# A hybrid decoder block on one core: weights rounded by casting DMAs, remainders made by accumulating DMAs

## The chip, the core and the metric

One NeuronCore of a Trainium2 chip runs the whole kernel. The time is device microseconds of one execution; a kernel's time is the median of several. Engines are named as in the profile: PE is TensorE, DVE is VectorE, ACT is ScalarE, POOL is GpSimd, and SP issues DMAs alone.

## The reference

One decoder layer works on 512 tokens of width 1024 (x is 512x1024, float32):

```python
h = rmsnorm(x, ln_mix_g)
aq, ak, av, iq, ik, iw, hq, hf, hi, hg, cb, cc, ch, gates = split(h @ w_in)
y_attn = sparse_attention(rms(aq), rms(ak), av, top-k by relu(iq @ ik) * iw, rel_bias)   # 8 heads of 64
y_hgrn = rms(gated_recurrence(hq, hf, hi)) * silu(hg)                                     # 4 heads of 128
y_conv = cb * causal_conv3(cc * ch)                                                       # 512 channels
mixed  = sum over b of sigmoid(gates[b]) * (y_b @ w_up_b)
x = x + mixed @ w_out
x = x + relu(rmsnorm(x) @ w_mlp_up)**2 @ w_mlp_down                                       # width 4096
```

All weights are float32 and the products are wanted at about that precision.

## The kernel before

**Products in three parts.** A float32 operand a is split into a rounded part (type `F32R`) and a remainder: a = hi + lo. Every large product is hi·hi + hi·lo + lo·hi, three matmuls that add into one accumulator bank. Activations are split where they are made (`xh`/`xl`, `x2h`/`x2l`, `hh`/`hl`, `mh`/`ml`, `yp`); weights are split on the way in.

**Slabs.** The weights are laid out in 142 slabs of up to 128x1024 floats (512 KB) in the order in which they are used (`PLAN`, `slabs_of`, lines 32 to 63): `kv` (three slabs), `hf`, `hq`, `hi`, `aq`, `cc`/`ch`/`cb`, `hg`, then for each branch the gates `g2`, `g1`, `g0` with the up-projections `u2`, `u1`, `u0`, then `wo`, and twice 16 slabs `up` and 16 slabs `dn`. A full slab feeds 24 matmuls of 512 columns. In the first stage (`start`, accumulators `Ast`) the weights of `iq` and of `hf` 0 come in by chunks of their own (`wst`) and are split in `first`; the change leaves that alone.

**How a slab comes in.** `loader` (line 394) has SP issue a DMA of the slab into a `raw` tile (two of them). `splitter` (line 440) lets ScalarE round it into a `whi` tile and VectorE subtract, `wlo = raw - whi` (three tiles of each). Then both are handed to the stream of matmuls under the key `("w", n)`, and freed when its last matmul is issued.

**How the order is made.** Each engine's instructions stand in an order that a planner writes down while the program is built (`Order`, line 95). Generators (`loader`, `splitter`, the evacuations `ev_*`, `scan_task`, `soft_task`, `out_task` and so on) yield operations with a cost in ns (`Op`), `Get` a tile, or `Need` a key. The main stream of matmuls (`main`: `start`, `cols`, `rows`, `tall`) advances the planner's clock; another generator's step is taken when the planner believes its inputs to be ready, and DMAs on SP count as ready 2000 ns after they end. So costs in the source decide where an instruction stands; each engine then runs its own list strictly in order and waits on semaphores.

**Names around the change.** `Akv`, `Ahf`, `Ag`, `Au`, `Awo`, `Aup`, `Adn` are accumulators of the stages; there are five banks for these. `xt` are four blocks of x in eight tiles, whose squares (`stats`) give the row norms `R`; every evacuation of a projection needs `R`. `iqs` is the split of the first two `Ast` banks, which are free only after it. In the scan, ScalarE makes an exponential `Am`, GpSimd multiplies it by `KQ` (`scan_task`, line 848), and TensorE uses it (`pa`, or by way of `prd` in `psum`). The attention adds bias and mask on GpSimd (`cmb`), makes logits (`pl`), transposes the probabilities `p` (`pt`) and multiplies by the values (`po`).

Of the kernel before, what the change touches and what calls it, by code (L numbers as in the profile page):

```python
# [11 lines left out]
F32 = mybir.dt.float32  # L12
F32R = mybir.dt.float32r
U32 = mybir.dt.uint32
I32 = mybir.dt.int32
AF = mybir.ActivationFunctionType
# [49 lines left out]
class Op:  # L66
    __slots__ = ("e", "c", "ins", "outs", "f")

    def __init__(self, e, c, ins, outs, f):
        self.e, self.c, self.f = e, c, f  # L70
        self.ins = [key(a) for a in ins if not isinstance(a, (int, float, type(None)))]
        self.outs = [key(a) for a in outs if a is not None]
# [22 lines left out]
class Order:  # L95
# [41 lines left out]
    def run(self, op):  # L137
# [3 lines left out]
        if op.e == "D":  # L141
            end += 2000
# [107 lines left out]
def kernel(ctx: ExitStack, tc: tile.TileContext, xT, x, wst, slabs, vecs, rel, ident_d, masks_d,  # L250
# [9 lines left out]
    def maker(pool, tag, shape, n):  # L260
# [6 lines left out]
        ("raw", sp, (128, 1024), 2), ("whi", sp, (128, 1024), 3), ("wlo", sp, (128, 1024), 3),  # L267
# [126 lines left out]
    def loader():  # L394
# [8 lines left out]
        for n in range(NSL):  # L403
            r = yield Get("raw", "raw")
            w = SLABS[n][2] * SLABS[n][4]
            yield dma(r[:, :w], slabs[n][:, :w], nbytes=1 << 19)
            put(("raw", n), r)
# [32 lines left out]
    def splitter():  # L440
        for n in range(NSL):
            r = yield Need(("raw", n))
            _, _, nk, _, nc_ = SLABS[n]
            w = nk * nc_
            h = yield Get("whi", "whi", F32R)
            yield act(h[:, :w], r[:, :w], AF.Copy)
            l = yield Get("wlo", "wlo", F32R)
            yield tt(l[:, :w], r[:, :w], h[:, :w].bitcast(F32), ALU.subtract)
            free(r)
            put(("w", n), (h, l, h[:, :w].rearrange("p (k c) -> p k c", k=nk), l[:, :w].rearrange("p (k c) -> p k c", k=nk)))  # L450
# [622 lines left out]
    def cols(n, m0, name, ev, rhs):  # L1073

        h, l, h3, l3 = yield Need(("w", n))
        nk, c = SLABS[n][2], SLABS[n][4]
        for mt in range((c + 127) // 128):
            w = min(128, c - 128 * mt)
            ps = yield Get("acc", "A" + name)
            cs = slice(128 * mt, 128 * mt + w)  # L1080
            for k in range(nk):
                yield Need(rhs[0](k))
                bh, bl = rhs[1](k)
                yield [mm(ps[:w], h3[:, k, cs], bh, k == 0, False), mm(ps[:w], h3[:, k, cs], bl, False, False),
                       mm(ps[:w], l3[:, k, cs], bh, False, k == nk - 1)]
# [3 lines left out]
    def rows(n0, cnt, name, ev, lhs, ncol):  # L1089
# [3 lines left out]
        for i in range(cnt):  # L1093
            h, l, h3, l3 = yield Need(("w", n0 + i))
# [49 lines left out]
    def tall(n, f, m):  # L1144
        ps = yield Get("acc", "Adn")
        for i in range(2):
            h, l, h3, l3 = yield Need(("w", n + i))
            for k in range(8):
                bh, bl = yield Need(("h", 16 * f + 8 * i + k))
                yield [mm(ps, h3[:, k], bh, i + k == 0, False), mm(ps, h3[:, k], bl, False, False),  # L1150
                       mm(ps, l3[:, k], bh, False, i == 1 and k == 7)]
# [129 lines left out]
```

## Time and profile before

| | |
|---|---|
| median of 3 runs | 888.13 us (886.86 to 889.04) |
| the profiled execution | 887.85 us, span of its instructions 886.1 us |
| TensorE matmul busy | 866.7 us (98%) |
| VectorE / ScalarE / GpSimd busy | 564.5 / 353.8 / 151.4 us |
| DMA | 88.08 MB, 100 GB/s over the span |

A page's busy time of an engine is the time in which at least one of its instructions ran. Matmuls overlap, so the start of one to the start of the next says more than the duration of one. The table by stretches gives for each engine the busy time and in brackets the number of instructions, then the granted clock of TensorE (1.00 is full), the share of time in which the 16 DMA engines were busy, and GB/s. A wait is shown as engine, line, and after the arrow what ended it.

### The profile page before, as it was taken

Reading aid. Unit: us, or ns where it says so; the run is one execution under the profiler, and the core shown is the slowest. Engines: PE = TensorE matmul, PEld = TensorE weight load, DVE = VectorE, ACT = ScalarE, POOL = GpSimd, SP = SyncE. Lnnn points to the kernel's source line nnn. Section 1 sums busy time; section 2 is a strip of 40 time slices with the busy share of each in tenths; the row PEclk is TensorE's granted clock in tenths of the full one; section 3 lists DMA queues with packets and bytes.
Section 4 is the critical chain, followed back from the end, with each engine's and each line's share of the span. In section 5 each row is a group of like instructions: output and inputs, shape, how many; then the busy total and the mean of one; then the engine's idle time right before and its main releaser. Section 6 shows DMA issues by size and latency. Waiting matters only on the chain.

```text
span 886.1 us, 10647 instructions
## 1 busy us (share of the span) xinstructions
PE 866.7 (98%) x4060; PEld 719.7 (81%) x4060; DVE 564.5 (64%) x972; ACT 353.8 (40%) x562; POOL 151.4 (17%) x129
## 2 busy tenths in 40 slices
PE   7999999998999999999999999999999999999997
PEld 6888888787888888888877888888888888888886
DVE  5589899999999996686557546444333344444331
ACT  6664354334433455565563333333222133331110
POOL 0010146445422421162200130000011100000000
PEclk9999999999999999999999999999999999999999
DMA  8443321222222222222221522223322222223330
GB/s 292 160 138 139 113 78 71 72 95 72 72 90 81 92 72 72 72 72 80 88 71 53 199 100 77 95 95 98 116 95 95 95 95 95 95 96 119 121 116 25
DMA packets 27611, 88.08 MB, mean 99 GB/s; under 512 B 2928, under 2 KB 5800, under 8 KB 27560
## 3 DMA queue, kind: packets, MB, share of 16 engines
q1 hardware_dynamic: 27528, 87.38, 29.0%
q8 instruction: 32, 0.52, 0.3%
q14 instruction: 19, 0.16, 0.1%
q0 software_dynamic: 32, 0.02, 0.0%
HBM read 85.28 MB, written 3.68 MB: 100 GB/s over the span
## 4 chain that ended last, share of the span: by engine, by line
PE 92%; DVE 6%; ACT 1%; DMA 0%; issue 0%; ACTq 0%; POOLq 0%
PE Aup L334 20%; PE Adn L334 20%; PE Ag L334 15%; PE Au L334 7%; PE Awo L334 5%; PE Aaq L334 2%; PE Ahq L334 2%; PE Ahi L334 2%; PE Ahf L334 2%; PE Ahg L334 2%; PE Ast L334 2%; PE pa L334 2%; PE Ach L334 2%; PE Akv L334 2%; PE Acc L334 1%; PE pl L334 1%
## 5 line engine op out<-in xcount | busy, mean ns | idle before, releaser
L296 ACT ACTIVATE whi<-raw 128x1024 fp32r<-128x1024 f32 (+2 forms) x150 | 153.8, 1026 | 276.9 <-PE Adn L334 124.5
L300 DVE TENSOR_TENSOR wlo<-raw,whi 128x1024 fp32r<-128x1024 f32 (+2 forms) x150 | 199.5, 1331 | 60.6 <-ACT whi L296 59.9
L334 PE MATMUL Aup<-x2h,whi 128*128 128x512 f32 x256 | 100.0, 391 | 0.0
L334 PE MATMUL Aup<-x2h,wlo 128*128 128x512 f32 x256 | 99.6, 389 | 0.0
L334 PE MATMUL Aup<-x2l,whi 128*128 128x512 f32 x256 | 99.6, 389 | 0.0
L334 PE MATMUL Adn<-hh,whi 128*128 128x512 f32 x256 | 99.6, 389 | 0.0
L334 PE MATMUL Adn<-hl,whi 128*128 128x512 f32 x256 | 99.6, 389 | 0.0
L334 PE MATMUL Adn<-hh,wlo 128*128 128x512 f32 x256 | 99.6, 389 | 0.0
L300 DVE TENSOR_TENSOR rl<-rl 128x512 f32<-128x512 f32 x32 | 22.2, 692 | 96.4 <-ACT hh L296 96.4
L334 PE MATMUL Ag<-xhi,whi 128*128 128x512 f32 x192 | 77.8, 405 | 0.0
L334 PE MATMUL Ag<-xhi,wlo 128*128 128x512 f32 x192 | 75.3, 392 | 0.0
L334 PE MATMUL Ag<-xlo,whi 128*128 128x512 f32 x192 | 75.0, 391 | 0.0
L334 PE MATMUL Au<-yp,whi 128*128 128x512 f32 x192 | 61.8, 403 | 2.3 <-ACT yp L296 2.1
L296 ACT ACTIVATE rl<-Aup 128x512 f32<-128x512 f32 x32 | 19.1, 598 | 110.2 <-PE Aup L334 110.2
L300 POOL TENSOR_TENSOR Am<-Am,KQ 128x512 f32<-128x512 f32 x28 | 43.5, 1554 | 97.0 <-ACT Am L296 92.0
L334 PEld LDWEIGHTS Aup<-x2h,whi 128*128 128x128 f32 x256 | 48.0, 188 | 10.3 <-issue 0.2
L334 PEld LDWEIGHTS Aup<-x2l,whi 128*128 128x128 f32 x256 | 48.1, 188 | 10.1 <-issue 0.2
L334 PEld LDWEIGHTS Adn<-hh,wlo 128*128 128x128 f32 x256 | 48.0, 188 | 10.0
L334 PEld LDWEIGHTS Adn<-hh,whi 128*128 128x128 f32 x256 | 48.0, 188 | 10.0
L334 PEld LDWEIGHTS Aup<-x2h,wlo 128*128 128x128 f32 x256 | 48.0, 188 | 9.9
L334 PEld LDWEIGHTS Adn<-hl,whi 128*128 128x128 f32 x256 | 48.0, 188 | 9.9
L334 PEld LDWEIGHTS Au<-yp,whi 128*128 128x128 f32 x192 | 35.8, 192 | 9.6 <-ACT yp L296 2.2
(261 smaller groups left out, 1702.9 us busy)
## 6 DMA issues: line engine op xcount, KB each, us to landing
raw<-in_slabs_dram SPq DMA_DIRECT2D x139, 512.0 KB, 3.2
xt<-in_x_dram SPq DMA_DIRECT2D x8, 256.0 KB, 6.5
x<-in_xT_dram SPq DMA_DIRECT2D x4, 512.0 KB, 5.8
out_dram<-o SPq DMA_DIRECT2D x7, 256.0 KB, 2.0
xin<-in_xT_dram SPq DMA_DIRECT2D x3, 512.0 KB, 6.0
d<-d SPq DMA_DIRECT2D x1, 1536.0 KB
raw<-in_wst_dram SPq DMA_DIRECT2D x3, 384.0 KB, 4.5
toep<-d SPq DMA_DIRECT2D x1, 1024.0 KB, 5.6
```

The costliest lines, as they stand in the source:

```text
L296: return Op("A", c, [in_, scale, bias], [out_, accum], lambda: A.activation(out_, in_, func, **kw))
L300: return Op(e, c, [a, b], [out_], lambda: (V if e == "V" else G).tensor_tensor(out_, a, b, op))
L334: return Op("PE", c, [a, b] + ([] if start else [ps]), [ps], lambda: PE.matmul(ps, a, b, start=start, stop=stop))
```

## The change

A slab's tile `raw` is gone. `loader` has GpSimd issue a DMA that reads the slab in DRAM as float32 and writes it into a `whi` tile as `F32R`, so that the rounding happens on the way. `splitter` hands that tile on at once under the key `("wh", n)`, lets ScalarE write the negated copy, `wlo = -whi`, and has GpSimd issue a second DMA of the same slab that adds into `wlo`, which makes it w - hi; this is handed on under `("wl", n)`. VectorE has no part in it. There are five tiles of each kind. `cols` and `tall` first do all products with the rounded weights of a slab and then those with the remainders; `rows` keeps its order. The planner books 900 ns on GpSimd for either DMA, and 3500 or 4000 ns more until it counts as landed. The scratch in SBUF for such DMAs' descriptors is made smaller (4096 bytes of a partition) to make room.

```diff
 class Op:
-    def __init__(self, e, c, ins, outs, f):
-        self.e, self.c, self.f = e, c, f
+    def __init__(self, e, c, ins, outs, f, lat=0):
+        self.e, self.c, self.f, self.lat = e, c, f, lat
...
-        if op.e == "D":
-            end += 2000
+        end += 2000 if op.e == "D" else op.lat
...
-        ("raw", sp, (128, 1024), 2), ("whi", sp, (128, 1024), 3), ("wlo", sp, (128, 1024), 3),
+        ("whi", sp, (128, 1024), 5), ("wlo", sp, (128, 1024), 5),
...
     def loader():
...
-            r = yield Get("raw", "raw")
+            h = yield Get("whi", "whi", F32R)
             w = SLABS[n][2] * SLABS[n][4]
-            yield dma(r[:, :w], slabs[n][:, :w], nbytes=1 << 19)
-            put(("raw", n), r)
+            yield Op("G", 900, [], [h], lambda h=h, n=n, w=w: nc.gpsimd.dma_start(h[:, :w], slabs[n][:, :w]), 3500)
+            put(("raw", n), h)
...
     def splitter():
         for n in range(NSL):
-            r = yield Need(("raw", n))
+            h = yield Need(("raw", n))
             _, _, nk, _, nc_ = SLABS[n]
             w = nk * nc_
-            h = yield Get("whi", "whi", F32R)
-            yield act(h[:, :w], r[:, :w], AF.Copy)
+            put(("wh", n), (h, h[:, :w].rearrange("p (k c) -> p k c", k=nk)))
             l = yield Get("wlo", "wlo", F32R)
-            yield tt(l[:, :w], r[:, :w], h[:, :w].bitcast(F32), ALU.subtract)
-            free(r)
-            put(("w", n), (h, l, h[:, :w].rearrange("p (k c) -> p k c", k=nk), l[:, :w].rearrange("p (k c) -> p k c", k=nk)))
+            yield act(l[:, :w], h[:, :w].bitcast(F32), AF.Copy, scale=-1.0)
+            yield Op("G", 900, [l], [l], lambda l=l, n=n, w=w: nc.gpsimd.dma_start(
+                l[:, :w], slabs[n][:, :w], accum_op=ALU.add), 4000)
+            put(("wl", n), (l, l[:, :w].rearrange("p (k c) -> p k c", k=nk)))
...
     def tall(n, f, m):
         ps = yield Get("acc", "Adn")
         for i in range(2):
-            h, l, h3, l3 = yield Need(("w", n + i))
+            h, h3 = yield Need(("wh", n + i))
             for k in range(8):
                 bh, bl = yield Need(("h", 16 * f + 8 * i + k))
-                yield [mm(ps, h3[:, k], bh, i + k == 0, False), mm(ps, h3[:, k], bl, False, False),
-                       mm(ps, l3[:, k], bh, False, i == 1 and k == 7)]
+                yield [mm(ps, h3[:, k], bh, i + k == 0, False), mm(ps, h3[:, k], bl, False, False)]
+            l, l3 = yield Need(("wl", n + i))
+            for k in range(8):
+                bh, _ = S["h", 16 * f + 8 * i + k]
+                yield [mm(ps, l3[:, k], bh, False, i == 1 and k == 7)]
             free(h, l)
...
-    nc = _bacc.Bacc("TRN2", target_bir_lowering=False, num_devices=1)
+    nc = _bacc.Bacc("TRN2", target_bir_lowering=False, num_devices=1, dynamic_dma_scratch_size=4096)
```

`cols` changes as `tall` does; where a slab has two tiles of output columns (`u0` to `u2`), both accumulators are open until the remainders have come.

**What moves.** The planner places everything anew. On TensorE, the last head of the attention (transposes `pt`, products `po`, tile numbers at the names' ends) stood in the middle of the first tile of the up-projection `u0` (`Au_769`):

```order
L334 MATMUL Au_769_4191<-yp_3741,wlo_4078 128x512
L334 MATMUL Au_769_4191<-yp_4064,whi_4076 128x512 x2
L334 MATMUL Au_769_4191<-yp_4064,wlo_4078 128x512
L339 MATMUL pt_4216<-ident,p_4037 128x128 x4
L339 MATMUL pt_4228<-ident,p_4037 128x128 x3
L334 MATMUL po_4215<-ph_4224,vst 128x512
L334 MATMUL po_4215<-pl_4225,vst 128x512
L339 MATMUL pt_4238<-ident,p_4037 128x128 x2
L339 MATMUL pt_4245<-ident,p_4037 128x128
L334 MATMUL po_4215<-ph_4232,vst 128x384
L334 MATMUL po_4215<-pl_4233,vst 128x384
```

Now the last products of the attention stand among matmuls of the gates of branch 1 (`Ag_641`), a stage earlier than `g0` and `u0`:

```order
L333 MATMUL Ag_641_3575<-xlo_229,whi_3286 128x512
L333 MATMUL po_3545<-ph_3592,vst 128x256
L333 MATMUL po_3545<-pl_3593,vst 128x256
L333 MATMUL Ag_641_3575<-xhi_236,whi_3286 128x512
L333 MATMUL Ag_641_3575<-xlo_254,whi_3286 128x512
L333 MATMUL Ag_641_3575<-xhi_263,whi_3286 128x512
L333 MATMUL Ag_641_3575<-xlo_286,whi_3286 128x512
L333 MATMUL po_3545<-ph_3605,vst 128x192
L333 MATMUL po_3545<-pl_3606,vst 128x192
L333 MATMUL Ag_641_3575<-xhi_110,wlo_3295 128x512
L333 MATMUL Ag_641_3575<-xhi_118,wlo_3295 128x512
L333 MATMUL Ag_641_3575<-xhi_137,wlo_3295 128x512
```

They have moved up past the rest of `g1`, all of `u1` and all of `g0`; in `u0` only its own products are left.

On ScalarE, at the program's start, from the fourth square of `xt` on, before:

```order
L296 ACTIVATE xt_157,ms_108<-xt_157 128x512
L296 ACTIVATE iqs_293<-Ast_103 64x384
L296 ACTIVATE iqs_295<-Ast_104 64x384
L296 ACTIVATE whi_288<-raw_260 128x648
L296 ACTIVATE xt_262,ms_108<-xt_262 128x512
L296 ACTIVATE iqs_308<-Ast_103 64x384
L296 ACTIVATE iqs_311<-Ast_104 64x384
L296 ACTIVATE xt_264,ms_108<-xt_264 128x512
L296 ACTIVATE xt_266,ms_108<-xt_266 128x512
L296 ACTIVATE xt_268,ms_108<-xt_268 128x512
L296 ACTIVATE whi_362<-raw_304 128x1024
```

and now, from the fifth square (here and below `wlo` from `whi` is the negated copy of a slab):

```order
L295 ACTIVATE xt_163,ms_108<-xt_163 128x512
L295 ACTIVATE wlo_278<-whi_161 128x648
L295 ACTIVATE xt_165,ms_108<-xt_165 128x512
L295 ACTIVATE xt_167,ms_108<-xt_167 128x512
L295 ACTIVATE xt_169,ms_108<-xt_169 128x512
L295 ACTIVATE iqs_301<-Ast_103 64x384
L295 ACTIVATE iqs_303<-Ast_104 64x384
L295 ACTIVATE wlo_307<-whi_171 128x1024
L295 ACTIVATE iqs_316<-Ast_103 64x384
L295 ACTIVATE iqs_320<-Ast_104 64x384
L295 ACTIVATE wlo_325<-whi_173 128x1024
```

The three copies of `whi` from `raw` have become copies of `wlo` from `whi`; all squares now stand ahead of both pairs of `iqs`, and the copy for slab 3 stands between the pairs.

On GpSimd, in the first head's levels of the scan (`X`, `prd`, `Am`), before:

```order
L326 MEMSET X_1034 128x512
L300 TENSOR_TENSOR prd_1043<-KQ_734 128x512
L300 TENSOR_TENSOR Am_1042<-Am_1042,KQ_734 128x2x256
L300 TENSOR_TENSOR prd_1070<-Am_1042 128x256
L300 TENSOR_TENSOR Am_1069<-Am_1069,KQ_734 128x2x128x2
L300 TENSOR_TENSOR prd_1106<-Am_1069 128x256 x2
L300 TENSOR_TENSOR Am_1132<-Am_1132,KQ_734 128x2x64x4
```

and now, with the DMAs of slabs between (`whi` is a cast into a free tile, `wlo` an accumulation):

```order
L325 MEMSET X_1042 128x512
L447 DMA wlo_1000<-in_slabs_dram 128x1024
L299 TENSOR_TENSOR prd_1057<-KQ_745 128x512
L299 TENSOR_TENSOR Am_1056<-Am_1056,KQ_745 128x2x256
L405 DMA whi_1092<-in_slabs_dram 128x1024
L299 TENSOR_TENSOR prd_1079<-Am_1056 128x256
L447 DMA wlo_1049<-in_slabs_dram 128x1024
L299 TENSOR_TENSOR Am_1087<-Am_1087,KQ_745 128x2x128x2
L299 TENSOR_TENSOR prd_1119<-Am_1087 128x256 x2
L405 DMA whi_1147<-in_slabs_dram 128x1024
L447 DMA wlo_1104<-in_slabs_dram 128x1024
L299 TENSOR_TENSOR Am_1129<-Am_1129,KQ_745 128x2x64x4
```

A pair of DMAs stands between products of the scan; in all there are 24 casts and 25 accumulations between the first `X` and the last `KQ` product.

## Rows read from the trace of the kernel before

**Rows 1.** The page, busy time of each engine, share of the span and instructions
```profile
PE 866.7 (98%) x4060; PEld 719.7 (81%) x4060; DVE 564.5 (64%) x972; ACT 353.8 (40%) x562; POOL 151.4 (17%) x129
```

**Rows 2.** Busy time by stretches; last three columns granted clock, DMA share, GB/s
```profile
core 0: us, PE busy (x) PEld busy (x) DVE busy (x) ACT busy (x) POOL busy (x), PEclk, DMA share, GB/s
0.00:22.10 22.10, 15.76 (x69) 14.55 (x70) 12.08 (x21) 14.64 (x27) 1.12 (x6) 1.00 0.84 292
54.40:64.40 10.00, 10.00 (x48) 8.36 (x47) 9.58 (x21) 7.90 (x14) 2.46 (x4) 1.00 0.54 195
110.00:310.00 200.00, 196.34 (x983) 162.36 (x982) 191.94 (x349) 80.39 (x116) 85.78 (x63) 1.00 0.24 82
460.00:472.50 12.50, 9.39 (x35) 6.39 (x34) 5.14 (x11) 3.28 (x9) 0.00 (x0) 0.86 0.13 43
553.80:575.90 22.10, 22.10 (x99) 18.32 (x98) 9.99 (x13) 8.26 (x12) 0.00 (x0) 1.00 0.29 95
```

**Rows 3.** Chain that ended last, in order of time: start us, us, what
```profile
620.38 87.04 PE Adn L334 x384
```

**Rows 4.** TensorE's waits: us in total, times, longest us
```profile
PE Ast L334 <- ACT xhi L296: 6.3, 1, 6.3
PE psum L334 <- DVE sl L300: 2.7, 2, 1.5
PE Au L334 <- ACT yp L296: 2.1, 1, 2.1
PE Akv L334 <- DVE iqs L300: 1.7, 1, 1.7
PE psum L334 <- DVE at L300: 0.7, 1, 0.7
```

**Rows 5.** TensorE's rows in order of time at the attention's end
```profile
460.48 0.88 PE L339 MATMUL pt<-ident,p 128*128 128x128 f32 x6 [0.16 <-ACT p L296]
...
469.61 0.63 PE L334 MATMUL Au<-yp,wlo 128*128 128x512 f32 x1
470.04 1.05 PE L334 MATMUL Au<-yp,whi 128*128 128x512 f32 x2
```

**Rows 6.** Rows in order of time at the start: ScalarE, VectorE, TensorE
```profile
22.19 0.86 ACT L296 ACTIVATE iqs<-Ast 64x384 fp32r<-64x384 f32 x2 [0.16 <-PE Ast L334]
...
24.32 0.86 ACT L296 ACTIVATE iqs<-Ast 64x384 fp32r<-64x384 f32 x2
...
26.52 0.63 ACT L296 ACTIVATE xt<-xt 128x512 f32<-128x512 f32 x1
...
30.33 1.06 ACT L296 ACTIVATE whi<-raw 128x1024 fp32r<-128x1024 f32 x1 [3.09 <-PE Akv L334]
...
22.71 1.01 DVE L300 TENSOR_TENSOR iqs<-Ast,iqs 64x384 fp32r<-64x384 f32 x2 [0.69 <-ACT iqs L296]
...
25.55 0.39 PE L334 MATMUL Akv<-whi,xhi 128*128 128x324 f32 x1 [1.68 <-DVE iqs L300]
```

**Rows 7.** DMA issues (KB each, median us to landing); SP in time; GB/s of 0 to 30 us
```profile
raw<-in_slabs_dram SPq DMA_DIRECT2D x139, 512.0 KB, 3.2
...
54.37 0.75 SPq L342 DMA_DIRECT2D d<-d  x1
...
64.58 0.39 SPq L342 DMA_DIRECT2D toep<-d  x1
...
GB/s 0 0 106 284 238 262 310 305 363 403 270 363 291 268 268 284 384 401 414 405 406 410 419 395 350 181 115 351 271 219 279 270 259 325 396 268 295 315 262 141
```

**Rows 8.** Groups of instructions: GpSimd, whole span; VectorE from 110 to 310 us
```profile
L300 POOL TENSOR_TENSOR Am<-Am,KQ 128x512 f32<-128x512 f32 x28 | 43.5, 1554 | 97.0 <-ACT Am L296 92.0 <-issue 5.0
L300 POOL TENSOR_TENSOR cmb<-toep,wk 128x256 f32<-128x256 f32 x24 | 18.1, 783 | 10.5 <-DVE os L308 10.5
L1197 POOL DMA_DIRECT2D vec<-in_vecs_dram x1 | 0.7, 699 | 0.8 <-POOLq L1269 0.8
...
L300 DVE TENSOR_TENSOR wlo<-raw,whi 128x1024 fp32r<-128x1024 f32 x30 | 47.5, 1584 | 0.0
```

More of the change, by code (lines that the diff above doesn't have):

```diff
@@ L66 @@
 class Op:
-    __slots__ = ("e", "c", "ins", "outs", "f")
-    def __init__(self, e, c, ins, outs, f):
-        self.e, self.c, self.f = e, c, f
+    __slots__ = ("e", "c", "ins", "outs", "f", "lat")
+    def __init__(self, e, c, ins, outs, f, lat=0):
+        self.e, self.c, self.f, self.lat = e, c, f, lat
         self.ins = [key(a) for a in ins if not isinstance(a, (int, float, type(None)))]
@@ L1073, in cols @@
     def cols(n, m0, name, ev, rhs):
-        h, l, h3, l3 = yield Need(("w", n))
+        h, h3 = yield Need(("wh", n))
         nk, c = SLABS[n][2], SLABS[n][4]
-        for mt in range((c + 127) // 128):
-            w = min(128, c - 128 * mt)
+        sl = [slice(128 * mt, min(c, 128 * mt + 128)) for mt in range((c + 127) // 128)]
+        pss = []
+        for cs in sl:
             ps = yield Get("acc", "A" + name)
-            cs = slice(128 * mt, 128 * mt + w)
+            pss.append(ps)
             for k in range(nk):
@@ L1083, in cols @@
                 bh, bl = rhs[1](k)
-                yield [mm(ps[:w], h3[:, k, cs], bh, k == 0, False), mm(ps[:w], h3[:, k, cs], bl, False, False),
-                       mm(ps[:w], l3[:, k, cs], bh, False, k == nk - 1)]
+                w = cs.stop - cs.start
+                yield [mm(ps[:w], h3[:, k, cs], bh, k == 0, False), mm(ps[:w], h3[:, k, cs], bl, False, False)]
+        l, l3 = yield Need(("wl", n))
+        for mt, (ps, cs) in enumerate(zip(pss, sl)):
+            for k in range(nk):
+                bh, _ = rhs[1](k)
+                yield [mm(ps[:cs.stop - cs.start], l3[:, k, cs], bh, False, k == nk - 1)]
             spawn(ev(m0 + mt, ps), 0)
@@ L1093, in rows @@
         for i in range(cnt):
-            h, l, h3, l3 = yield Need(("w", n0 + i))
+            h, h3 = yield Need(("wh", n0 + i))
+            l, l3 = yield Need(("wl", n0 + i))
             kk = h3.shape[1]
```

## The prediction

> **What bounds the kernel now.** I read the page's busy times first: TensorE is busy for 866.7 of 886.1 us, VectorE for 564.5 and GpSimd for only 151.4 [rows 1]. The chain of waits says what that busy time is worth: 384 matmuls of 512 columns take 87.04 us [rows 3], so 0.2267 us each, back to back. A slab of weights (24 such matmuls) is therefore 5.44 us of TensorE, and no change of weight preparation makes that less. What can be won is idle time. The list of TensorE's waits shows where it lies [rows 4]: 6.3 us before the first matmul, 1.7 us at the start of `kv`, 3.4 us in two waits for VectorE inside the scan (2.7 and 0.7), and the waits around the attention's end, of which 2.1 us is the longest.
>
> The last place costs more than its waits. Between 460.0 and 472.5 the table by stretches counts 35 TensorE rows [rows 2]: 17 matmuls of `Au` (17 x 0.2267 = 3.85 us), eight of `po` (2688 columns together, 1.19 us at the same pace) and ten transposes (0.88 us for six [rows 5], 1.47 us for ten). That is 6.5 us of work in 12.5, so **6.0 us** are lost. Part of them is the clock: it was granted at 0.86 there [rows 2], so some of the stretch ran at the lower of the two levels (1.2 and 2.4 GHz); after the stop of 2.1 us one matmul takes 0.43 us (469.61 to 470.04 [rows 5]), twice the usual. The mean costs 0.14 x 12.5 = 1.7 us of the 6.0.
>
> Before that, from 110 to 310 us, VectorE is the fullest helper: 191.9 of 200 us, of which 30 remainders take 47.5 us [rows 2, 8]. GpSimd had 85.8 us.
>
> **The change part by part.** Durations are from the profiled execution, 887.85 us (span 886.1 and 1.75 around it); the median of the three runs is 888.13, 0.3 us more.
>
> *VectorE loses the remainders.* 142 subtractions go; in the scan's stretch that is 47.5 us of 191.9. VectorE is not the bound, so the gain is only what TensorE waited for it. But the planner sees the freed time and draws the attention forward: its last `po` now stands among the gate matmuls of `g1` (`Ag_641`), not at the end of `u0`. Nothing of the attention stands at the old place, so the 6.0 us go: **-6.0**. The last attention head is now hidden by the 1.5 gate and product stages behind it; without that cover the 6.0 stay. Of the 3.4 us in the scan I take half, **-1.7**, between none and all, since the same stretch now holds the attention too.
>
> *ScalarE* keeps its count: a negated copy of 128x1024 replaces the rounding copy of 128x1024, same size, 1.06 us [rows 6], cost 0. But its order at the start changes. Before, the second pair of `iqs`, which gives `kv` its third accumulator bank, stood ahead of three squares of `xt`; TensorE went on at 25.55 [rows 6]. Now all eight squares and the copy for slab 3 stand ahead of it: 3 x 0.63 + 1.06 = 3.0 us more [rows 6], if no load is late.
>
> *The loads at the start.* The five casts are issued at once, beside the 5.90 MB that SP loads (by the code 1536 KB of `wst`, 2048 of `xT`, 2048 of `x`, 128 of constants); before, slab loads stood between those in SP's one queue. The DMA engines are already busy at 0.84 in the first 22.1 us, moving 292 GB/s [rows 2], so 348 at full share; single slices reach 419 [rows 7]. The last square of `xt` now needs 5.90 MB and the casts' 2.38 behind it at even sharing, and two accumulating loads that start meanwhile. With these as one plain load each (1.05 MB): 9.33 MB / 348 GB/s = 26.8, and 1.5 us until the first bytes: 28.3. Then a square (0.63), a pair of `iqs` (0.86), the copy (1.06), half a pair and a subtraction (0.5) [rows 6], 3.5 us: TensorE goes on at 31.8, which is +6.3. With accumulating loads three times as dear it is +12.3. At 400 GB/s the loads are in by 24.8 and ScalarE's order alone counts, +3.0. I take the middle of 3.0 and 6.3, +4.7, and for the clock after so long a stop the 1.7 us of the attention's end: **+6.4**, between 3.0 and 14.0.
>
> The Trainium skill (DMA: Bandwidth & Descriptors, Queues, rings and completion order) says that each DMA engine alternates between the queues it has work for, packet by packet. By that the casts would take half the engines from SP's loads as soon as they are queued, and this term would be its even-sharing value, 6.3 + 1.7 = 8.0, and the sum 891.6 us; no row here shows two busy queues.
>
> *GpSimd* gets 285 issues in all, 284 of them new. The only row is that of `vec`: 0.70 us [rows 8]. In the scan an issue stands ahead of nearly every `Am` product, and a cast waits for TensorE to leave slab n-5, so what is queued behind waits too, and TensorE for that. From the first `X` to the last `KQ` there are 49 issues, 34 us at 0.70. Against that, `Am` products found GpSimd idle for 97.0 us before them [rows 8], so most is hidden. I take a tenth, **+3.4**; bounds 0 (all hidden) and 34 (none).
>
> *DMA in the steady stages.* A plain slab takes a 0.29 share of 5.44 us [rows 2], 1.58 us. The cast I price as one such load. The accumulation also reads SBUF. The nearest row that reads and writes as much is the 1536 KB broadcast in DRAM: from 54.4 to 64.4 the share was 0.54 with one slab in it, so (5.4 - 1.58) / 3 = 1.27 us for each 512 KB [rows 2, 7]. So an accumulation costs one load or little more; I bound it by one and three. Up to 2.4 loads (1 / 0.29 - 1) it fits beside the matmuls: cost **0**. A cast may be issued five slabs ahead, 27.2 us; landing twice (3.2 us each [rows 7]), two issues and a copy take some 9 us, and TensorE asks for the remainder only after 16 rounded products. If this cover goes, every slab pays.
>
> The Trainium skill (Collectives: The Full Stack, Part 3) says that an add in the DMA path costs twice a copy because it has two source reads, not because of the adding. By that the share would be 0.29 + 0.58 = 0.87 and this term still 0; 1.27 us for read and write together is less than it would say, though for a copy.
>
> *At nothing:* the order of products (same matmuls at the same pace), the buffers (raw out, five and five in), and the smaller descriptor scratch. SP loses its slab loads, so its other transfers only come earlier.
>
> Sum: -6.0 - 1.7 + 6.4 + 3.4 = +2.1, so 887.85 + 2.1 = **890.0 us**, 0.2% over the median: no change that can be told. About 0.3% (2.7 us) is what a measurement can tell from none.
>
> **Rivals.**
> *The start stays short (faster).* Transfers speed up as more are queued, GpSimd's issues hide: -6.0 - 3.4 + 3.0 = -6.4, 881.5 us. For it: the slices of 419 GB/s and the idle 97 us. Against: ScalarE's order is 3.0 whatever the loads do.
> *GpSimd becomes the bound of the scan (slower).* The stretch from first `X` to last `KQ` holds 24 casts; at before's 200 us for 31 slabs it lasts 155 us. GpSimd's own work there is 85.8 and 9.4 us of the attention's 12 additions (783 ns each [rows 8]). That leaves 60 us for 49 issues: from 1.2 us an issue on it decides. At 1.5 us it costs 15 in place of 3.4: 901.6 us. Against: 0.70 in the one row, and no more contention with remainders on VectorE.
> *The DMA engines become the bound (slower).* If an accumulation takes over 2.4 loads; at three, a slab takes 6.3 us, some 0.9 more for each of 139: about 1010 us. Against: the 1.27 us above.
> *The attention's gap only moves,* because the denser middle runs late: then the first term is 0 and the time 896.
>
> **How the numbers follow.** My sum 0.35 (with its bounds: same 0.20, slower 0.12, faster 0.03); short start 0.30 (faster 0.27, same 0.03); GpSimd 0.14 (slower 0.12, same 0.02); DMA 0.09, slower; moved gap 0.12 (slower 0.11, same 0.01). Together: faster 0.30, same 0.26, slower 0.44. The sum's own range runs from 885 to 899 us. The range reaches from the short start, 880, to GpSimd as the bound, 904, and leaves out the DMA case and the worst starts.
>
> **What would show it.** Right: TensorE goes on with `kv` between 28 and 34 us, no stop near 460, a DMA share of 0.55 to 0.9 in the up and down stages with matmuls still at 0.227 us, issue rows on GpSimd below 1.2 us. Wrong: TensorE waiting for `wlo` in the up stage (then the DMA engines), or for `Am`, `prd` or `cmb` in the scan (then GpSimd), or a `kv` start as early as before.

## The result, and the profile after

The changed kernel takes **906.91 us** (median of 4 runs, 906.26 to 908.14) against 887.91 us (886.86 to 889.04): a ratio of 1.0218, with an interval from 1.0201 to 1.0234. It is slower by 2.2%, and 2.9 us above the range that was forecast. The profiled execution has a span of 904.4 us (886.1 before).

The page of the changed kernel: busy times, the DMA share in 40 slices, the DMA queue that GpSimd fills, and the issues (KB each, median us to landing).

```profile
PE 873.5 (97%) x4060; PEld 723.4 (80%) x4060; DVE 414.1 (46%) x830; ACT 361.6 (40%) x562; POOL 340.4 (38%) x413
...
DMA  9789888656656455478999988899889998999981
...
q0 software_dynamic: 40928, 148.44, 75.4%
...
L405 POOL DMA_DIRECT2D whi<-in_slabs_dram x142 | 84.5, 596 | 298.0 <-PE Aup L333 107.2
L447 POOL DMA_DIRECT2D wlo<-in_slabs_dram x142 | 126.8, 893 | 179.1 <-ACT wlo L295 162.2
...
whi<-in_slabs_dram POOLq DMA_DIRECT2D x139, 512.0 KB, 5.1
wlo<-in_slabs_dram POOLq DMA_DIRECT2D x139, 512.0 KB, 7.3
```

VectorE is 150 us less busy than in [rows 1], GpSimd 189 us more, with 211 us of DMA issues in it, 0.60 and 0.89 us each. TensorE has the same 4060 instructions and 7 us more of busy time, a sign of a lower clock somewhere. The table by stretches of the changed kernel shows where (its granted clock is the number before the DMA share), beside [rows 2]:

```profile
0.00:22.10 22.10, 13.30 (x56) 11.24 (x57) 8.99 (x17) 11.26 (x19) 4.62 (x12) 1.00 0.94 337
22.10:40.00 17.90, 12.55 (x63) 11.27 (x62) 6.19 (x19) 11.61 (x27) 3.68 (x5) 0.81 0.94 206
110.00:310.00 200.00, 192.22 (x983) 158.73 (x982) 183.65 (x365) 97.05 (x163) 131.58 (x133) 0.97 0.66 142
360.00:396.00 36.00, 32.78 (x153) 26.01 (x153) 16.21 (x44) 19.67 (x44) 7.31 (x10) 0.95 0.59 139
553.80:575.90 22.10, 22.10 (x97) 17.96 (x96) 8.91 (x10) 9.16 (x12) 6.44 (x9) 1.00 0.87 189
```

In the up stage (last row) TensorE is busy without a break at a DMA share of 0.87, and the chain has 384 matmuls of a later stage in the 87.04 us of [rows 3]:

```profile
638.95 87.04 PE Adn L333 x384
```

The losses lie ahead of it: at the start, in the scan, and at 360 to 396 us, where the attention now ends. In the scan's stretch the 47.5 us of remainders [rows 8] are gone, yet VectorE is busy for 183.65 us in place of 191.94: only 8.3 us came free. TensorE's waits in the changed kernel (us in total, times, longest):

```profile
PE Ast L333 <- ACT xhi L295: 10.0, 4, 5.7
PE Akv L333 <- DVE iqs L299: 3.5, 1, 3.5
PE po L333 <- DVE pl L299: 3.0, 2, 2.8
PE po L333 <- ACT ph L295: 2.9, 2, 2.0
PE pl L333 <- DVE at L319: 2.3, 1, 2.3
PE pt L338 <- ACT p L295: 1.4, 1, 1.4
```

Of [rows 4] the waits of `psum` are gone; new are those of the attention (`pl`, `po`, `pt`) and three in the first stage (`Ast`), where x itself comes in later. At the start TensorE's rows show the stop before `kv` and the slow rows behind it:

```profile
28.52 0.31 PE L333 MATMUL Akv<-whi,xlo 128*128 128x324 f32 x1
32.30 0.61 PE L333 MATMUL Akv<-whi,xhi 128*128 128x324 f32 x1 [3.47 <-DVE iqs L299]
32.71 0.47 PE L333 MATMUL Akv<-wlo,xhi 128*128 128x324 f32 x1
```

`kv` goes on at 32.30, not at 25.55 [rows 6]. From 32.3 to 36.9 a matmul of 324 columns starts every 0.27 us, later every 0.147: that is the lower clock level (0.81 is the mean from 22.1 to 40.0), about 2 us more.

**Losses by stretch.** To compare kernels whose orders differ, I take for each TensorE row the time from its start to the next row's start, less the pace of its shape in the kernel before (0.227 us for 512 columns, 0.147 for 324). Summed, 852.6 us are work in every kernel here, and some 5 us follow the start of the last matmul; what is left is lost (us, from the profiled executions):

| kernel | until the first matmul | 0 to 60 | scan, 120 to 300 | attention, 300 to 490 | median us |
|---|---|---|---|---|---|
| before | 6.3 | 5.2 | 7.7 | 9.6 | 887.9 |
| changed | 5.7 | 14.7 | 16.4 | 10.4 | 906.9 |
| e1_order_kept | 6.4 | 15.0 | 4.5 | 13.1 | 898.7 |
| e2_no_accumulation | 5.5 | 12.8 | 13.3 | 1.5 | 893.1 |
| e3_old_start | 6.1 | 6.1 | 15.3 | 1.4 | 889.4 |
| e4_relief_alone | 6.0 | 6.5 | 4.9 | 1.9 | 877.3 |
| e5_no_issues | 6.4 | 9.5 | 9.8 | 1.4 | 888.3 |
| e6_later_copies | 6.9 | 14.9 | 22.8 | 4.2 | 907.6 |
| e7_start_and_later | 6.1 | 6.0 | 17.7 | 1.8 | 891.7 |
| e8_half_relief | 5.7 | 7.8 | 11.4 | 2.6 | 886.8 |
| e9_small_accumulation | 6.1 | 14.4 | 15.0 | 2.5 | 898.0 |
| e10_relief_after_scan | 5.9 | 6.7 | 6.2 | 8.6 | 886.3 |
| e11_relief_after_scan_later | 6.2 | 7.5 | 8.9 | 3.5 | 883.5 |
| e12_products_on_vector | 6.5 | 6.8 | 3.7 | 2.6 | 878.3 |

Elsewhere no kernel loses over 0.7 us. Changed against before: the start +8.9, the scan +8.7, the attention +0.8.

**Part of it is the clock.** In the profiled execution of the changed kernel the clock is granted at 0.50 from 30.1 to 36.9 us, from 204.2 to 207.6, from 241.8 to 248.6 and from 392.0 to 395.4; each time TensorE was standing or had just stood (for 3.47, 2.29, 2.77 and 1.96 us). The longest stop of the scan and the rows behind it, which start 0.42 us apart and not 0.227:

```profile
242.54 0.79 PE L333 MATMUL po<-ph,vst 128*128 128x512 f32 x1 [2.77 <-DVE pl L299]
243.56 0.63 PE L333 MATMUL Ahg<-xhi,whi 128*128 128x512 f32 x1
243.98 0.63 PE L333 MATMUL Ahg<-xlo,whi 128*128 128x512 f32 x1
```

Such slow rows make 8.2 us of the changed kernel's loss (2.2 at the start, 4.5 in the scan, 1.5 at the attention's end) and 1.6 of the loss before. So over a third of the 18 us is lost not in the stops but in slow rows around and behind them. How many there are varies: over the four executions the mean clock was 0.988 to 0.992, and the one at 0.988 was the quickest, so it isn't shown that the time would fall by as much without them.

### The profile page after: what moved, and what is told of

The parts are those of the page before. It is cut to its first block, busy times and chain, and to the rows that moved or that the text cites. A ratio compares the mean times of both kernels' runs of the same rounds, so it can differ in the third digit from the quotient of the medians.

```text
span 904.4 us, 10733 instructions
## 1 busy us (share of the span) xinstructions
PE 873.5 (97%) x4060; PEld 723.4 (80%) x4060; DVE 414.1 (46%) x830; ACT 361.6 (40%) x562; POOL 340.4 (38%) x413
## 4 chain that ended last, share of the span: by engine, by line
PE 81%; issue 7%; DVE 6%; DMA 3%; POOL 2%; ACT 1%; SPq 0%; POOLq 0%; ACTq 0%
PE Aup L333 19%; PE Adn L333 19%; PE Ag L333 10%; PE Awo L333 5%; PE Au L333 5%; PE Aaq L333 2%; PE Ahq L333 2%; PE Ahi L333 2%; PE Acc L333 2%; DMA xt<-in_x_dram 2%; PE Acb L333 2%; PE Ach L333 2%; PE Ahf L333 2%; PE Akv L333 2%; PE Ahg L333 2%
## 5 line engine op out<-in xcount | busy, mean ns | idle before, releaser
L295 ACT ACTIVATE wlo<-whi 128x1024 fp32r<-128x1024 f32 (+1 forms) x142 | 149.8, 1055 | 312.3 <-DMA whi<-in_slabs_dram 281.2
L405 POOL DMA_DIRECT2D whi<-in_slabs_dram x142 | 84.5, 596 | 298.0 <-PE Aup L333 107.2
L447 POOL DMA_DIRECT2D wlo<-in_slabs_dram x142 | 126.8, 893 | 179.1 <-ACT wlo L295 162.2
L299 DVE TENSOR_TENSOR rl<-rl 128x512 f32<-128x512 f32 x32 | 22.1, 690 | 124.2 <-ACT hh L295 124.2
L333 PE MATMUL Aup<-x2h,wlo 128*128 128x512 f32 x256 | 63.8, 391 | 0.0
L333 PE MATMUL Adn<-hh,wlo 128*128 128x512 f32 x256 | 63.2, 389 | 0.0
L333 PEld LDWEIGHTS Aup<-x2h,wlo 128*128 128x128 f32 x256 | 48.1, 188 | 10.4 <-issue 0.5
L333 PE MATMUL Ag<-xhi,wlo 128*128 128x512 f32 x192 | 51.0, 395 | 0.0
L333 PE MATMUL Au<-yp,whi 128*128 128x512 f32 x192 | 47.7, 393 | 0.0
L299 DVE TENSOR_TENSOR X<-X 128x256 f32<-128x256 f32 x56 | 42.9, 766 | 3.3 <-ACT Am L295 2.2
```

Of the source, the lines that this page charges most:

```text
L295: return Op("A", c, [in_, scale, bias], [out_, accum], lambda: A.activation(out_, in_, func, **kw))
L299: return Op(e, c, [a, b], [out_], lambda: (V if e == "V" else G).tensor_tensor(out_, a, b, op))
L333: return Op("PE", c, [a, b] + ([] if start else [ps]), [ps], lambda: PE.matmul(ps, a, b, start=start, stop=stop))
L405: yield Op("G", 900, [], [h], lambda h=h, n=n, w=w: nc.gpsimd.dma_start(h[:, :w], slabs[n][:, :w]), 3500)
L447: yield Op("G", 900, [l], [l], lambda l=l, n=n, w=w: nc.gpsimd.dma_start(l[:, :w], slabs[n][:, :w], accum_op=ALU.add), 4000)
```

## The experiments

**Three undone parts, and the relief alone.** The first question was whether the freed VectorE was spent by the planner, eaten by GpSimd, or lost to traffic.

**e1_order_kept**, in `splitter`, ahead of the accumulation:

```diff
+            yield Op("V", 1.0 * (145 + 1.05 * w), [l], [], lambda: None)
```

> The changed kernel, with VectorE's subtraction still booked in the planner but not issued: the attention's place stays near the old one. Theory 1 (the freed VectorE time was spent by drawing the attention forward, so VectorE stays the bound of the scan): the time lost on TensorE from 120 to 300 us falls from 15.6 us to 7 or less, a stop near 450 to 470 comes back with some 6 us, the start stays; 891 to 896 us in all. Theory 2 (GpSimd's issues stand in front of the scan's products): the scan's loss stays at 13 or more, 904 to 910 us. Theory 3 (DMA traffic slows the middle): the same as theory 2.

Measured: 898.65 us, ratio 1.0119 (1.0102 to 1.0137), over what theory 1 gave. (The 15.6 us in the text is the table's 16.4, reckoned a little differently.) The scan's loss fell to 4.5 with all issues and traffic in place, and the stops at the attention's end came back, but with 13.1 us, spread from 380 to 460. So what VectorE is booked for, and with it where the attention stands, decides what the scan loses; the late place now costs more than before's 9.6.

**e2_no_accumulation**, in `splitter`:

```diff
-            yield Op("G", 900, [l], [l], lambda l=l, n=n, w=w: nc.gpsimd.dma_start(
-                l[:, :w], slabs[n][:, :w], accum_op=ALU.add), 4000)
+            yield Op("G", 900, [l], [l], lambda: None, 4000)
```

> The changed kernel without the accumulating DMAs (planned but not issued), in the same order of everything else; it leaves the remainder out, wlo stays -whi. Theory 3 (traffic): the start gets 4 to 6 us shorter and the scan's loss of 15.6 us at least halves, below 896 us; the DMA share of the up stage falls from 0.92 to about 0.4. Theory 2 (issues on GpSimd): half of the issues go, the scan's loss falls by 3 to 6 us. Theory 1: the scan's loss and the stops at the attention's end stay within 3 us of the changed kernel's, and only the start gains, 898 to 902 us.

Measured: 893.13 us, ratio 1.0061 (1.0044 to 1.0078). No theory had this: the scan kept most of its loss (13.3), the start gained 2, and the attention's 10.4 us fell to 1.5. All but 1.5 us of what the attention's end lost came with the accumulations. The table by stretches of this kernel (scan, attention, up stage):

```profile
110.00:310.00 200.00, 193.70 (x1012) 160.79 (x1011) 180.19 (x372) 100.37 (x173) 107.79 (x110) 0.99 0.23 72
300.00:490.00 190.00, 190.00 (x905) 158.53 (x904) 78.26 (x190) 86.87 (x157) 37.29 (x55) 1.00 0.28 90
553.80:575.90 22.10, 22.10 (x99) 18.32 (x98) 5.54 (x8) 9.17 (x12) 2.12 (x4) 1.00 0.31 96
```

**e3_old_start**, in `loader`; in `splitter` these three slabs get the rounding copy and the subtraction of the kernel before:

```diff
+            if n < 3:
+                r = yield Get("wlo", "raw")
+                yield dma(r[:, :w], slabs[n][:, :w], nbytes=1 << 19)
+                put(("raw", n), r)
+            else:
+                if n == 3:
+                    tick = ct([128, 1], "tick")
+                    yield cp(tick, r[:, :1], "G")
...
```

> The changed kernel with its first three slabs (kv) loaded by SP and split by ScalarE and VectorE as before, and the casts from slab 3 on held back on GpSimd until the third of them has landed. If the start costs 8.8 us because casts and accumulations share the DMA engines with SP's loads, kv goes on at 25 to 27 us in place of 32.3 and the time falls by 7 to 9 us, to 898 to 900 us. If ScalarE's order alone makes the start late, it falls by 3 or less.

Measured: 889.39 us, ratio 1.0019 (1.0007 to 1.0031). The start lost 6.1 in place of 14.7. This kernel undoes two things there, the casts and accumulations among SP's loads and ScalarE's new order; e5 below parts them. The time fell by 17.5, not by 7 to 9: the attention's end went from 10.4 to 1.4 as well. From slab 3 on the accumulations are all there, a cast still takes some 5.8 us to land, and from 300 to 396 us ScalarE still stands for 17.9 us in all in front of copies whose cast has not landed (23.7 in the changed kernel). But the planner has placed those copies otherwise: every `ph` of that stretch is ready 0.8 us or more before TensorE's `po` starts, while in the changed kernel two are ready only 0.05 us before. So traffic alone does not make that loss; it needs an order that is tight.

**e4_relief_alone**, on the kernel before, in `splitter`:

```diff
+            if n < 5:
+                yield tt(l[:, :w], r[:, :w], h[:, :w].bitcast(F32), ALU.subtract)
+            else:
+                yield act(l[:, :w], r[:, :w], AF.Copy, scale=-1.0)
-            yield tt(l[:, :w], r[:, :w], h[:, :w].bitcast(F32), ALU.subtract)
```

> The kernel before with VectorE's subtraction replaced, from slab 5 on, by a second copy on ScalarE (negated): no DMA on GpSimd, VectorE as free as in the changed kernel; it leaves the remainder out, wlo is -w. Theory 1: the attention is drawn forward here too and VectorE stays the bound, so the scan loses 10 us or more and the time is 884 to 892 us, little or no gain. Theory 2 or 3: without issues and traffic the relief shows, the scan loses less than 5 us and the stop near 460 goes, 872 to 880 us.

Measured: 877.28 us, ratio 0.9882 (0.9867 to 0.9897). This speaks against theory 1: with VectorE free, the attention drawn forward, and no DMA on GpSimd, the scan loses 4.9 and the attention 1.9, and VectorE has time to spare. But it is another order than the changed kernel's: the last `po` stands in `g0`, between before's `u0` and the changed kernel's `g1`. The row of the scan:

```profile
110.00:310.00 200.00, 199.04 (x1041) 166.64 (x1040) 169.17 (x370) 123.89 (x190) 88.70 (x79) 1.00 0.22 77
```

**One order, four ways to load.** The next two kernels and e2_no_accumulation keep the changed kernel's order: TensorE, ScalarE, VectorE and GpSimd run the same instructions in the same sequence in all four, the DMAs' issues apart.

**e5_no_issues**, in `loader`; in `splitter` the copy serves as both weight parts, and the accumulation is planned but not issued:

```diff
-            yield Op("G", 900, [], [h], lambda h=h, n=n, w=w: nc.gpsimd.dma_start(h[:, :w], slabs[n][:, :w]), 3500)
+            yield Op("G", 900, [], [h], lambda h=h, n=n, w=w: nc.sync.dma_start(h[:, :w], slabs[n][:, :w]), 3500)
```

> The changed kernel's order kept as the planner wrote it, but each slab comes by one plain load that SP issues, ScalarE's negated copy of it serves as the rounded part too, and no cast or accumulation is issued; it leaves the remainder out, both weight operands are the rounded -w. Theory A (GpSimd's issues and what they wait for hold the scan back): the loss from 120 to 300 us falls from 16.4 us (13.3 without accumulations) to 7 or less and VectorE's time there falls by over 8 us; with a start as before, 878 to 883 us. Theory B (the order with the attention drawn forward is itself too tight for VectorE): the loss stays at 11 or more, 886 to 890 us.

Measured: 888.30 us, ratio 1.0005 (0.9994 to 1.0017); its profiled execution is the quickest of ten, so its losses in the table are some 1.8 us low against this median. TensorE also reads ScalarE's copy in place of the landed slab here, but none of the waits that the profile lists for it is for a copy. The scan's 9.8 lie between the two theories: the order by itself loses 2 more than before and 5 more than e4's, and GpSimd's DMAs make 16.4 of it. The start's 9.5 are the order too: `kv` goes on at 28.21, 2.7 us later than before, behind a stop of 3.99 us for `iqs`, with 1.7 us of slow rows behind it.

**e9_small_accumulation**, in `splitter`:

```diff
-                l[:, :w], slabs[n][:, :w], accum_op=ALU.add), 4000)
+                l[:, :8], slabs[n][:, :8], accum_op=ALU.add), 4000)
```

> The changed kernel with each accumulating DMA cut to 8 columns of a slab: the same issue, behind the same copy, on GpSimd, but next to no traffic; it leaves out the remainder of all other columns. The accumulations cost the changed kernel 8.9 us at the attention's end (10.4 lost against 1.5 in e2_no_accumulation), 3.1 in the scan and 2.0 at the start. If they cost by standing in GpSimd's queue and waiting there for ScalarE's copy, the attention's end still loses 8 us or more and the scan 16: 901 to 905 us. If they cost by their traffic, which makes the casts land later and so ScalarE's copies and what stands behind these, the attention's end loses under 3 us and the scan 13 to 14: 892 to 896 us.

Measured: 897.97 us, ratio 1.0118 (1.0104 to 1.0133). With the issues there but no traffic, the attention's end loses 2.5; the start stays at 14.4 and the scan at 15.0. Its issues take as long as those of whole slabs:

```profile
L447 POOL DMA_DIRECT2D wlo<-in_slabs_dram x142 | 128.4, 905 | 111.1 <-ACT wlo L295 93.5
```

This makes a ladder, by medians: the order 888.3 (e5); casts issued by GpSimd +4.8 (e2); the accumulations' issues +4.8 (e9); their traffic **+8.9** (changed). By the table the casts and the accumulations' issues (e5 to e9) cost 4.9 us at the start, 5.2 in the scan and 1.1 at the attention's end; the last step lies at the attention's end (7.8 of it). Slow rows are in the steps: 1.7 us in e5, 3.1 in e2, 4.3 in e9, 8.2 in the changed kernel.

In the scan the traces show one way in which the issues cost time. The stop at 242.54 above stands at the same place of the order in all four kernels and is 1.02 us in e5, 2.10 in e2, 2.77 in e9 and in the changed kernel. Ahead of it VectorE has an instruction of 4 columns, `os`, and GpSimd the attention's additions `cmb`. In e5 and then in the changed kernel:

```profile
231.90 0.59 DVE L312 SCALAR_TENSOR_TENSOR os<-os 128x4 f32<-128x4 f32 x1
230.86 2.29 POOL L299 TENSOR_TENSOR cmb<-toep,wk 128x256 f32<-128x256 f32 x3
```

```profile
239.55 2.33 DVE L312 SCALAR_TENSOR_TENSOR os<-os 128x4 f32<-128x4 f32 x1
239.42 2.44 POOL L299 TENSOR_TENSOR cmb<-toep,wk 128x256 f32<-128x256 f32 x3
```

The issues ahead of `cmb` make it start later against VectorE's work (1.04 us ahead of `os` in e5, 0.13 in the changed kernel), so `os` now lasts until the additions are through (both end at 241.9), and `pl` and TensorE wait behind it.

At the attention's end the traces say how the traffic costs. DMA issues from 360 to 396 us (KB each, us to landing), first without accumulations (e2), then in the changed kernel:

```profile
whi<-in_slabs_dram POOLq DMA_DIRECT2D x6, 512.0 KB, 3.5
```

```profile
wlo<-in_slabs_dram POOLq DMA_DIRECT2D x5, 512.0 KB, 5.4
whi<-in_slabs_dram POOLq DMA_DIRECT2D x4, 512.0 KB, 6.8
```

GpSimd, ScalarE and TensorE of the changed kernel in order of time there:

```profile
382.58 0.87 POOL L447 DMA_DIRECT2D wlo<-in_slabs_dram  x1 [6.89 <-ACT p L295]
383.13 0.89 POOL L405 DMA_DIRECT2D whi<-in_slabs_dram  x1
...
385.08 0.60 ACT L295 ACTIVATE ph<-pt 128x512 fp32r<-128x512 f32 x1 [0.75 <-PE pt L338]
390.23 1.06 ACT L295 ACTIVATE wlo<-whi 128x1024 fp32r<-128x1024 f32 x1 [4.55 <-DMA whi<-in_slabs_dram]
391.20 0.47 ACT L295 ACTIVATE ph<-pt 128x384 fp32r<-128x384 f32 x1
...
391.72 0.51 PE L333 MATMUL po<-ph,vst 128*128 128x384 f32 x1 [1.96 <-ACT ph L295]
```

The cast goes out right behind an accumulation, both are under way together, and it lands after 7 us. ScalarE stands for 4.55 us in front of the negated copy, and the attention's `ph` waits behind it; TensorE's `po` waits for that `ph`. The next longest stops there, 1.43 us until 356.69 and 0.96 until 375.23, come the same way, behind copies that ScalarE began after 2.53 and 4.60 us of standing. From 300 to 396 us it stood so for 23.7 us in all, in e9 for 0.5. The copy was not urgent: remainders land 16 to 28 us before their first matmul there (accumulations issued from 280 to 395 us, landing against TensorE's rows).

**Moving the copies, and moving the attention.**

**e6_later_copies**, in `loader` and `splitter`:

```diff
-            yield Op("G", 900, [], [h], lambda h=h, n=n, w=w: nc.gpsimd.dma_start(h[:, :w], slabs[n][:, :w]), 3500)
+            yield Op("G", 900, [], [h], lambda h=h, n=n, w=w: nc.gpsimd.dma_start(h[:, :w], slabs[n][:, :w]), 3500 if n < 5 else 8000)
...
-                l[:, :w], slabs[n][:, :w], accum_op=ALU.add), 4000)
+                l[:, :w], slabs[n][:, :w], accum_op=ALU.add), 4000 if n < 5 else 8000)
```

> The changed kernel with one number changed: from slab 5 on the planner counts a cast or an accumulation as landed 8000 ns after its issue (3500 and 4000 before), so that the negated copy and the accumulation's issue stand later on ScalarE and GpSimd. Theory A': at the attention's end GpSimd stands still in front of each accumulation until the cast has landed and ScalarE has copied, with the attention's mask additions behind it; then the 10.4 us lost from 300 to 490 fall to under 4 and the scan's 16.4 by some us, 892 to 898 us. Rival: the additions are late because GpSimd is slow in any order; then the loss stays at 8 or more, 903 to 908 us.

Measured: 907.62 us, ratio 1.0223 (1.0206 to 1.0240). The attention's loss fell to 4.2, and ScalarE no longer stands in front of its copies there, but the scan's loss rose to 22.8, and the time is the changed kernel's. The theory was right for the attention and missed the time: the waits move, and this order has no better place for them.

**e7_start_and_later** has the edits of e3_old_start and of e6_later_copies:

```diff
+            if n < 3:
+                r = yield Get("wlo", "raw")
...
+                l[:, :w], slabs[n][:, :w], accum_op=ALU.add), 4000 if n < 5 else 8000)
```

> The first three slabs loaded the old way (as in e3_old_start) and the later landing times of e6_later_copies together. If the waits of GpSimd for casts are part of what the scan loses, its 15.3 us of e3_old_start fall to 8 to 11, and the time to 882 to 886 us; if only the bunching of GpSimd's own work counts, it stays within 2 us of e3_old_start's 889.4.

Measured: 891.69 us, ratio 1.0051 (1.0036 to 1.0066): 2.3 above e3, the scan at 17.7. So later places for copies and accumulations do not help the scan; neither forecast was met.

**e8_half_relief**, on e7_start_and_later, in `splitter`:

```diff
+            yield Op("V", 0.5 * (145 + 1.05 * w), [l], [], lambda: None)
```

> e7_start_and_later with half of the subtraction's time still booked for VectorE in the planner (nothing is issued for it), so that the attention is drawn forward only half as far. If the scan loses because VectorE is booked full while GpSimd lengthens its instructions, the scan's loss falls to 5 to 8 us without a new stop at the attention's end: 876 to 881 us, faster than both kernels. If the place of the attention has no part in it, the same as e7_start_and_later.

Measured: 886.77 us, ratio 0.9993 (0.9984 to 1.0003). The scan's loss fell from 17.7 to 11.4, some half of what was expected, and the time is 6 us over the forecast. The place of the attention, or what else moves when VectorE is booked for half, does count.

**e10_relief_after_scan**, on e3_old_start, in `splitter`:

```diff
+            if 0 <= n < 40:
+                yield Op("V", 1.0 * (145 + 1.05 * w), [l], [], lambda: None)
```

> e3_old_start with the subtraction's whole time booked for VectorE in the planner up to slab 39 (nothing issued for it) and none after it: the scan is planned as if VectorE were as full as before, the attention is drawn forward only behind it. By the sum of e1_order_kept's scan (4.5 us lost), e3's start (6.1) and attention's end as in e3 (1.4 to 4): 852.6 of work, 6.1 until the first matmul, 12 to 15 lost, 871 to 876 us, faster than both. If the attention's end loses 13 as in e1_order_kept, 881 to 885 us.

Measured: 886.31 us, ratio 0.9982 (0.9971 to 0.9994): the scan at 6.2, but the attention's end at 8.6, in between the two cases, and the time over both.

**e11_relief_after_scan_later** has the edits of e10_relief_after_scan and of e6_later_copies:

```diff
+            if 0 <= n < 40:
+                yield Op("V", 1.0 * (145 + 1.05 * w), [l], [], lambda: None)
...
+                l[:, :w], slabs[n][:, :w], accum_op=ALU.add), 4000 if n < 5 else 8000)
```

> e10_relief_after_scan with the later landing times of e6_later_copies. If ScalarE's and GpSimd's waits for casts are what holds the attention's end, it loses less there than e10 and the time is 1 to 4 us under it; if the scan loses more again, as it did from the changed kernel to e6 (6.4 us more), it is 3 to 6 us over it.

Measured: 883.52 us, ratio 0.9953 (0.9939 to 0.9968): with the scan relieved, the later copies do what they were meant to, 3.5 at the attention's end, though the scan loses 2.7 more. One long stop was left in the scan, from 213 us on. TensorE's row behind it, then VectorE and GpSimd of this kernel ahead of it:

```profile
217.81 0.80 PE L333 MATMUL pss<-hi,kd 128*128 128x128 f32 x2 [4.42 <-ACT kd L295]
```

```profile
203.43 4.28 DVE L299 TENSOR_TENSOR os<-os 128x4 f32<-128x4 f32 x1
207.63 0.41 DVE L319 COPY at<-pa 64x256 f32<-64x256 f32 x1
207.97 2.95 DVE L319 COPY dec<-X 128x4 f32<-128x4 f32 x1
```

```profile
202.76 1.34 POOL L299 TENSOR_TENSOR aq<-aq,qr 128x512 f32<-128x512 f32 x1
203.77 1.57 POOL L299 TENSOR_TENSOR u<-u,zc 128x512 f32<-128x512 f32 x1
205.01 2.67 POOL L299 TENSOR_TENSOR KQ<-KQ,X 128x1024 f32<-128x1024 f32 x1
...
208.97 1.92 POOL L299 TENSOR_TENSOR prd<-KQ 128x512 f32<-128x512 f32 x1
```

An instruction of 4 columns, 0.15 us elsewhere, lasts 4.28 us, until three products on GpSimd are through; `dec` ends with the next one, `prd`. From there VectorE works without a pause until what `kd` needs is done. So the last run took such products from GpSimd.

**e12_products_on_vector**, on e11, in `scan_task` (and the same in `q_task` for the scaling of `aq`):

```diff
-            yield tt(KQ, KQ, X, ALU.mult, "G")
+            yield tt(KQ, KQ, X, ALU.mult)
```

> e11_relief_after_scan_later with two kinds of GpSimd's products moved to VectorE: KQ times X (128x1024, 2.39 us on GpSimd, four times) and the scaling of aq (128x512, 1.30 us, four times). In e11 the small instructions os and dec on VectorE last 4.2 and 2.9 us around 204 to 211 us, just as long as these products run beside them, and TensorE then stands for 4.6 us. If VectorE's instructions wait for GpSimd's, the eight moved products (8 of some 1 us) cost VectorE no more than the waits that go, the scan's loss falls from 8.9 us to 4 to 6 and the time to 878 to 881 us. If the long rows are only coincidence, VectorE gets 8 us more to do and the scan loses as much as in e11 or more, 884 to 890 us.

Measured: **878.26 us**, ratio 0.9898 (0.9882 to 0.9915): 1.0% faster than the kernel before and 3.2% faster than the changed one, with nothing left out. The scan loses 3.7 us. VectorE got eight products more and is less busy from 110 to 310 us, 157.19 us against 161.22 in e11; `dec` fell from a mean of 1631 ns to:

```profile
L319 DVE COPY dec<-X 128x4 f32<-128x4 f32 x4 | 0.6, 159 | 0.0
```

Two rivals stay open. The move also frees GpSimd and makes the planner place everything anew (the last `po` is at 450 us, 436 in e11), so not all of the 5.3 us need be the shorter rows. And the kernel before was not run with these products moved, so how much of the 1.0% is owed to the DMAs isn't shown.

## Why the prediction was wrong

Three terms came out dearer than forecast, and nothing made up for it: the attention's end +0.8 in place of -6.0, the scan +8.7 in place of +1.7 (-1.7 and +3.4), the start +8.9 in place of +6.4. Together that is +18.4 in place of +2.1. Two of the prediction's rivals added up in its own prices, a moved gap (0) and GpSimd as the bound (+15), give 0 - 1.7 + 6.4 + 15 = +19.7 and 907.6 us, close to the 906.9 measured, but that is luck: the scan lost 4.6 us less than these prices say and the start 2.5 more, and neither rival's reason held. The issues stayed under the 1.2 us from which GpSimd was to be too full, and the denser middle by itself (e5) loses only 1.4 at the attention's end.

All four signs of being right came: `kv` went on at 32.30, the stop near 460 went, the share was 0.87 with matmuls at 0.227 us, and issues took 0.60 and 0.89 us. None of them asked what the attention's new place or the scan would lose.

- **"Nothing of the attention stands at the old place, so the 6.0 us go": the first step that failed.** The stop near 460 went, as forecast, but the attention lost 10.4 us at its new place. In the changed order without issues or traffic the loss goes from 9.55 to 1.44, -8.1 (e5); issues gave back 1.1 and the accumulations' traffic 7.8. Which instruction stands ahead of the last `ph` on ScalarE, and what that one waits for, was in the order and was not asked.
- **"Scan -1.7" and "GpSimd +3.4": the second step that failed.** It let the relief gain something and hid nine tenths of the issues' time in GpSimd's idle time. The relief alone gives -2.7 (7.66 to 4.92, e4), somewhat more than forecast. But the changed order loses +2.1 against before (e5), for which the sum had no term; the casts and issues add 5.2 (e5 to e9) and the accumulations' traffic 1.4. Of the scan's 16.4 us, 4.5 are slow rows at the lower clock, for which the scan had no price. The ladder's 9.7 us for the issues (893.13 - 888.30 and 897.97 - 893.13) are those of the whole kernel, and some half of them lie at the start. The issue rows were 0.60 and 0.89 us, near the 0.70 assumed, so GpSimd was not too full: it is what stands in its queue, and when, that costs.
- **What VectorE kept.** The unasked question was how much of the 47.5 us it would keep: only 8.3 came free. Part went to the attention drawn in (365 instructions for 349, the 30 remainders gone), part to longer rows. Over the quickest tenth of their form VectorE's rows of that stretch took some 34 us more before, 50 in the changed kernel, 35 in e4, 40 in e5 and 24 in e12. Of the 50 us, 46 lie in the 193 rows that overlapped a product of GpSimd. That longer rows make TensorE wait is seen at the stop at 242.54 of the changed kernel and at the one from 213 us in e11, which e12 does not have; how far they explain the whole 6.6 us stays open.
- **"Start +6.4", between 3.0 and 14.0: the mechanism right, the size low.** It is +8.9 (9.5 more lost in the first 60 us, and the first matmul 0.6 earlier). `kv` went on at 32.30, 6.75 later than before; even sharing gave 31.8 and +6.3. ScalarE's order alone was to be +3.0 and is +2.7 in e5. The sum took the middle of the two, +4.7, where the upper value was the right one. The slow rows behind the stop cost about 2 us, forecast 1.7. The value by the Trainium skill (DMA: Bandwidth & Descriptors, Queues, rings and completion order), 8.0, was nearer.
- **"DMA 0" held where it was looked for:** matmuls at 0.227 us at a share of 0.87 in the up stage, 0.3 us lost behind 490. An accumulation adds 0.87 - 0.31 = 0.56 (e2), 1.8 times a cast's 0.31. The Trainium skill (Collectives: The Full Stack, Part 3) has an add at twice a copy, which is near; that its 0.87 came out to the digit is luck, since the cast was 0.31 and not 0.29 and the add less than double. No run here shows the reason. The term failed for the whole kernel: what lands late holds a matmul of its own slab only once (0.7 us at the start), but it holds a copy with others behind it.

## What to carry to other kernels

A DMA moved to an engine that computes brings its waits into that engine's queue, and into the queue of whoever copies its result: read what stands right behind each, not only how long the issue takes. When a planner is told that an engine has become free, it spends that at once, and the gain can turn into another tight place. Booking a longer landing paid here only once the scan had been relieved (e11 against e10, not e6 or e7). Price a new order by itself, as in e5, before pricing what is issued in it; and let rivals happen together, but check each one's reason before their sum is believed.

## What the runs showed of the hardware

An instruction on VectorE that reads SBUF can stand until GpSimd's product is through. In the changed kernel both rows start at 190.13 and end together (VectorE first):

```profile
190.13 1.30 DVE L299 TENSOR_TENSOR os<-os 128x4 f32<-128x4 f32 x1
```

```profile
190.13 1.29 POOL L299 TENSOR_TENSOR Am<-Am,KQ 128x512 f32<-128x512 f32 x1 [2.66 <-ACT Am L295]
```

The Trainium skill (SBUF — State Buffer, SBUF: two separate sides) says that the two share a pair of ports, which one holds for its whole instruction while the other blocks, where VectorE's operation has two inputs in SBUF or runs in a two-port mode. The rows of `os`, with two inputs in SBUF, agree, and `dec`, a copy, fell from 1631 to 159 ns when products left GpSimd; no run here shows the ports themselves. In e12 VectorE took over eight products and was still busy for 4.0 us less from 110 to 310 us, in a stretch that holds more of TensorE's work (1019 rows for 986). GpSimd's DMA issues alone hardly lengthened VectorE's rows: the 68 that overlapped an issue and no product from 110 to 310 us took 2.2 us more in all than the quickest of their forms. And an accumulating issue takes 0.9 us whatever it moves (0.905 at 4 KB, 0.893 at 512 KB).
